# Input projection of a hybrid decoder layer in seven block products for pairs of column tiles, with attention in groups of two query blocks

## The chip, the core and the metric

The kernel runs on one core of a Trainium2 chip. The core's engines each follow their own queue and meet through semaphores: PE (TensorE) multiplies, DVE (VectorE), ACT (ScalarE) and POOL (GpSimd) work elementwise, SP issues DMA transfers. The metric is the device time of one execution in microseconds, the median of the runs.

## The reference, cut to what matters

One layer for 1024 prompt tokens and 32 sample tokens (8 sequences of 4), all in float32. `w_in` has 9472 columns, 74 tiles of 128.

```python
u = rmsnorm(x, norm_pre)
proj = jnp.einsum('bld,de->ble', u, w_in)
aq, af, ai, aog, az, bq, bk, bv, bz, ga, gb = jnp.split(proj, offs, axis=-1)
# branch A: gated linear recurrence, 8 heads of 128 channels
oa, s_new = hgrn2_branch(aq, af, ai, aog, s_hgrn, lb, hgrn_norm)
a = jnp.einsum('ble,ed->bld', oa * silu(az), w_pa)
# branch B: attention over a window of 128, 16 heads, 2 key heads, a sink per head
b = jnp.einsum('ble,ed->bld', swa(bq, bk, bv) * silu(bz), w_pb)
m = sigmoid(ga) * a + sigmoid(gb) * b
x = x + rmsnorm(jnp.einsum('bld,de->ble', m, w_o), norm_post)
x = x + (p @ w_ple) * sigmoid(x @ w_ple_gate)
```

The recurrent states, and the last 128 keys and values, are outputs too.

## The kernel before

Activations lie transposed, channels on partitions: a projection's tile of 128 output columns is a product over eight channel tiles (k). For float32 accuracy each operand is split exactly into a rounded part and a rest (`wh`, `wl`, `uH`, `uL`, type fp32r), and three products are added for each k: wh x uH, wh x uL, wl x uH. `gemm` (line 245 issues all its products) does this for three chunks of 352 tokens, 24 products into one of three PSUM banks each, so 72 a tile; the sample's 32 tokens are the end of the third chunk. The first head's first two tiles run in chunks of 256, 256, 256 and 288 while the tokens still arrive. `weights` loads a tile of 1024 x 128, rounds it on ACT (L216) and subtracts on DVE (L217).

PE's order is written out by hand. Dependent work stands in generators in two queues; `gemm` calls `tick` after each quantum of products (8; 4 in attention), and `tick` lets the first generator of each queue go on to its next `yield`, which says how many quanta it waits. The other engines' orders come from the framework's planner, which starts what is ready and prefers what was written earlier; at run time each engine keeps that order.

The stages: the norm and the turning of the input (`x_rest`, `turn`); for each of eight heads five tiles (f, q, i, og, z) with the head's chain beside them (`hgrn_proj`, `hgrn_chain`, and `turn_v` for the values): pairs of tokens in blocks of 4, 16 and then halves of 32, 64, 128 (L573 to L636), states (L674, L691), outputs (L703, L705), squares (L707), scaled outputs (L717, L718), their transposes (L732). The chain's PSUM is two double banks (`double`) and one single bank (`single`); the values of the sample are spread over sequences by POOL (L686). Then keys and values, with `turn_kv` beside the values' projection; eight gates of branch A in turn with its output projection (`gate_a`, `ep_pa`); for each of eight tiles (two heads each) bq and bz with `attention` beside them; the sample's attention; eight gates of branch B; its projection and the merge; the output projection, post norm, residual and the layer input.

`attention` takes a tile in two halves of four query blocks: logits of two blocks (L884, L888) with the reduction that adds the bias (L893), softmax of four blocks (L904, L909), transposes of the probabilities into two banks `pt` (L929, copies L933 and L935), values into a bank `po` (L956), gating (L962). Its steps wait `A_WAIT` quanta.

Of the kernel before, what the change touches and what calls it, by code (L numbers as in the profile page):

```python
# [11 lines left out]
F32 = mybir.dt.float32  # L12
# [15 lines left out]
A_QUANTUM = 4  # L28
A_WAIT = (5, 4, 4, 5, 5, 4, 3, 3, 3, 3)
# [10 lines left out]
# column offsets of the parts of the input projection  # L40
# [3 lines left out]
# layout of the constant tile (columns)  # L44
# [6 lines left out]
C_SM = 344  # L51
# [10 lines left out]
def _constants():  # L62
    """Tables that depend on shapes alone: identity, masks, one-hot rows of the distance buckets."""
# [3 lines left out]
    # the ten (source, target) pairs of a block of four: columns t=1..3 with s=t, t=2,3 with s=t-1, t=3 with s=1,  # L67
    # and t=0..3 with s=0; then the same of four blocks of four in one of sixteen, and of two halves of 32
# [13 lines left out]
    c[:32, C_VM:C_VM + 8] = tok[:, None] // 4 == np.arange(8)[None, :]  # L82
    b = _buckets()
# [8 lines left out]
    # one-hot rows of the buckets along the reversed distance axis, and a row for what is masked  # L92
# [4 lines left out]
    # the same for the four sample positions: row (t, bucket), column key  # L97
# [14 lines left out]
def tile_decoder_step(ctx: ExitStack, tc: tile.TileContext, x_prompt, x_sample, state_hgrn, cache_k, cache_v,  # L112
# [13 lines left out]
    wp = ctx.enter_context(tc.tile_pool(name="wp", bufs=2))  # L126
    ep = ctx.enter_context(tc.tile_pool(name="ep", bufs=2))
    dp = ctx.enter_context(tc.tile_pool(name="dp", bufs=1, space=DRAM))
    psg = ctx.enter_context(tc.tile_pool(name="psg", bufs=3, space=PSUM))

# [1 line left out]
    oa_d = [dp.tile([P, NTOK], F32, name=f"oa_d{h}") for h in range(NH)]  # L132
    ma_d = [dp.tile([P, NTOK], F32, name=f"ma_d{h}") for h in range(KT)]
# [4 lines left out]
    cst = cp.tile([P, C_W], F32, name="cst")  # L138
# [7 lines left out]
    def rsqrt_steps(dst_i, src, scale, tag, pool_):  # L146
        """dst_i (an int32 tile, read as float32) = (src * scale + EPS) ** -0.5, an instruction a step"""
# [23 lines left out]
    # ---- the order of work on the tensor engine: projections in quanta of a few products, with the steps of  # L171
    # ---- dependent work (generators in queues) between them; a step yields how many quanta to wait, or a condition
# [30 lines left out]
    wn = [0]  # L203

    def weights(srcs, kt=KT, split=True):
        i = wn[0]
        wn[0] += 1
        raw = wp.tile([P, NTOK], F32, name=f"raw{i}", tag="raw")
        raw3 = raw[:, :kt * P].rearrange("p (k m) -> p k m", k=kt)
        for dst, src in srcs:  # L210
            DM.dma_start(dst(raw3), src)
        wh = wp.tile([P, KT, P], F32R, name=f"wh{i}", tag="wh")
        wl = wp.tile([P, KT, P], F32R, name=f"wl{i}", tag="wl")
        if not split:
            return wh, wl, raw3
        S.copy(wh[:, :kt, :], raw3)  # L216
        V.tensor_tensor(wl[:, :kt, :], raw3, wh[:, :kt, :], op=ALU.subtract)  # L217
        return wh, wl

    def w_cols(src, col, kt=KT, split=True):  # L220
        return weights([(lambda r: r, src[:, col:col + P].rearrange("(k p) m -> p k m", p=P))], kt, split)

    def w_strips(src, base, c):
        out = []
        for j in range(2):
            col = base + (c + 8 * j) * 64
            out.append((lambda r, j=j: r[:, :, 64 * j:64 * j + 64], src[:, col:col + 64].rearrange("(k p) m -> p k m", p=P)))
        return weights(out)

    def w_rows(i):  # L230
        return weights([(lambda r, j=j: r[64 * j:64 * j + 64],
                         w_pb[0, 512 * j:512 * j + 512, i * P:(i + 1) * P].rearrange("(k p) m -> p k m", p=64)) for j in range(2)])

    gn = [0]

    def gemm(w, xh, xl, epilogue, kt=KT, chunks=CHUNKS, quantum=8):
        wh, wl = w
        n = 0
        for lo, hi in chunks:
            gn[0] += 1  # L240
            ps = psg.tile([P, 512], F32, name=f"g{gn[0]}", tag="g")[:, :hi - lo]
            sl = slice(lo, hi)
            for k in range(kt):
                for m, (a, b) in enumerate(((wh, xh), (wh, xl), (wl, xh))):
                    T.matmul(ps, a[:, k, :], b(k)[:, sl], start=k == 0 and m == 0, stop=k == kt - 1 and m == 2)  # L245
                    n += 1
                    if n % quantum == 0 and not (k == kt - 1 and m == 2):
                        tick()
            epilogue(lo, sl, ps)
            tick()  # L250
# [4 lines left out]
    # =====================================================================================  # L255
    # input norm, transposed: u^T in two exact float32r parts
    # =====================================================================================
    ap_, ap_es = opened("ap")
    uHt = ap_.tile([P, KT, NTOK], F32R, name="uH", tag="AH")
    uLt = ap_.tile([P, KT, NTOK], F32R, name="uL", tag="AL")  # L260
    uH, uL = rows(uHt), rows(uLt)

    st, st_es = opened("st")
    sps, sps_es = opened("stps", bufs=5, space=PSUM)
    done = set()
    rawt = ep.tile([P, NTOK], F32, name="rawt", tag="ep")
    raws = [rawt[:24, i * P:(i + 1) * P] for i in range(2)]
    rs_i = st.tile([P, 9], I32, name="rs_i", bufs=1)
    tabs = st.tile([P, 2], F32, name="tabs", bufs=1)
    xts = []  # L270

    def load_x(i):
        r = P if i < 8 else 32
        xt = st.tile([P, D], F32, name=f"xt{i}", tag="xt", bufs=7)
        DM.dma_start(xt[:r], x_prompt[0, i * P:(i + 1) * P, :] if i < 8 else x_sample.rearrange("b t d -> (b t) d"))
        xts.append((xt, r))

    # the start's order is by hand on the other engines too
    first = ExitStack()
    first.enter_context(tc.manual_schedule(engines={mybir.EngineType.Activation, mybir.EngineType.DVE, mybir.EngineType.Pool}))  # L280
    one = rawt[:, 768:896]
# [10 lines left out]
    first_w = [w_cols(w_in[0], O_AF, split=False)]  # L292
    load_x(2)
    first_w.append(w_cols(w_in[0], O_AQ, split=False))
    for i in range(3, 9):
        load_x(i)
    DM.dma_start(cst[:, P:], cst_d[:, P:])
    DM.dma_start(sink, attn_sink.broadcast_to([P, 16]))

    def split_w(i):  # L300
        wh, wl, raw3 = first_w[i]
        S.copy(wh, raw3)
        for hf in range(2):
            k = slice(4 * hf, 4 * hf + 4)
            G.tensor_tensor(wl[:, k], raw3[:, k], wh[:, k], op=ALU.subtract)

    def squares(i):
        xt, r = xts[i]
        sq = st.tile([P, D], BF16, name=f"sq{i}", tag="sq")
        S.activation(sq[:r], xt[:r], AF.Square, accum_out=ssq[:r, i:i + 1])  # L310

    def chain(i, n):
        return rsqrt_steps(rs_i[:, i:i + n], ssq[:, i:i + n], 1.0 / D, f"u{i}", st)
# [15 lines left out]
    def turn(p, q, beside=()):  # L329
        """two of the eight channel tiles of a pair of token tiles, times the norm's weight"""  # L330
# [6 lines left out]
        dst = slice(256 * p, 256 * p + 256)  # L337
        gs = [g_pre[:, 2 * q + k:2 * q + k + 1] for k in range(2)]
        for k in range(2):
            S.activation(uHt[:, 2 * q + k, dst], pt[:, k, :], AF.Copy, scale=gs[k])  # L340
# [968 lines left out]
```

## Time and profile before

| | |
|---|---|
| median of 3 runs | 1566.18 us (1565.2 to 1570.24) |
| span of the profiled execution | 1565.5 us |
| one head (from 165.5 to 239.8 us) | 74.3 us |
| one tile of attention (from 861.0 to 897.3 us) | 36.3 us |
| gates and projection of branch A (651.3 to 848.0) | 196.7 us |

A group's line names the source line, engine, operation, output and inputs, shapes and count; behind the bar stand busy time and the mean duration of one in ns, then idle time ahead of them and who ended it. Matmuls overlap in PE, so the distance from start to start says what one costs, and its duration does not. A timeline's line begins with start and duration in us. A window's line gives the stretch, each engine's busy time with its instructions, PE's granted clock, the DMA engines' share and GB/s. A line of waits gives total us, times and the longest.

### The profile page before, as it was taken

How to read it: one execution, taken by the hardware profiler on the slowest of the kernel's cores; microseconds unless marked ns; L12 is line 12 of the kernel's file. 1: busy time of each engine (PE TensorE's matmuls, PEld its weight loads, DVE VectorE, ACT ScalarE, POOL GpSimd, SP SyncE). 2: the span in 40 equal slices, each digit the busy share in tenths (PEclk: the TensorE clock that was granted, in tenths of full speed). 3: DMA queues.
4: the chain of work that ended last, by engine and by line, in shares of the span. 5: the costliest groups of instructions: out<-in, count | busy, mean ns of one | idle time of the engine just before them, and what ended most of it. 6: DMA issues, size and time to landing. Idle time of an engine off the chain costs nothing.

```text
span 1565.5 us, 28202 instructions
## 1 busy us (share of the span) xinstructions
PE 1542.4 (99%) x11799; PEld 1477.2 (94%) x11799; DVE 765.1 (49%) x1875; ACT 520.5 (33%) x1257; POOL 133.6 (9%) x98
## 2 busy tenths in 40 slices
PE   8999999999999999999999999999999999998998
PEld 8999999999999999999999888888999999997998
DVE  7746464646455564421213666666524344227532
ACT  6342323332323323511113444444324112323422
POOL 2211010202020202200000000000000000004100
PEclk9999999999999999999999999999999999998999
DMA  6121212121212121522222111111222454203321
GB/s 201 55 70 42 79 33 84 42 70 42 83 31 82 30 82 31 177 76 69 76 62 75 35 39 39 46 35 37 68 76 76 138 134 127 67 13 117 94 82 56
DMA packets 181578, 112.24 MB, mean 72 GB/s; under 512 B 40003, under 2 KB 174076, under 8 KB 181436
## 3 DMA queue, kind: packets, MB, share of 16 engines
q1 hardware_dynamic: 180636, 110.21, 24.3%
q8 instruction: 92, 1.51, 0.4%
q14 instruction: 34, 0.28, 0.1%
q0 software_dynamic: 672, 0.18, 0.1%
q10 hardware_dynamic: 144, 0.07, 0.0%
HBM read 88.22 MB, written 23.22 MB: 71 GB/s over the span
## 4 chain that ended last, share of the span: by engine, by line
PE 87%; DVE 5%; DMA 3%; issue 2%; ACT 1%; SPq 0%; DVEq 0%; ACTq 0%
PE g L245 72%; DMA mar<-ma_d 3%; PE po L956 2%; PE pt L929 2%; PE lp L884 1%; DVE wl L217 1%; PE d L463 1%; PE d L703 1%; PE d L674 1%; PE lp L888 1%; PE d L705 1%; DVE mL L1112 1%; PE d L573 1%; PE b L636 1%; DVE gbr L1110 0%
## 5 line engine op out<-in xcount | busy, mean ns | idle before, releaser
L245 PE MATMUL g<-uH,wh 128*128 128x352 f32 (+2 forms) x1792 | 583.6, 326 | 0.0
L245 PE MATMUL g<-uL,wh 128*128 128x352 f32 (+2 forms) x1792 | 580.4, 324 | 0.0
L245 PE MATMUL g<-uH,wl 128*128 128x352 f32 (+2 forms) x1792 | 579.6, 323 | 0.0
L245 PEld LDWEIGHTS g<-uL,wh 128*128 128x128 f32 x1792 | 337.9, 189 | 8.8 <-issue 5.2
L245 PEld LDWEIGHTS g<-uH,wh 128*128 128x128 f32 x1792 | 337.4, 188 | 9.3 <-issue 7.2
L245 PEld LDWEIGHTS g<-uH,wl 128*128 128x128 f32 x1792 | 337.5, 188 | 6.2 <-issue 3.4
L217 DVE TENSOR_TENSOR wl<-raw,wh 128x1024 fp32r<-128x1024 f32 (+1 forms) x112 | 135.3, 1208 | 228.2 <-ACT wh L216 228.1
L216 ACT CAST wh<-raw 128x1024 fp32r<-128x1024 f32 (+1 forms) x112 | 112.2, 1002 | 289.8 <-PE g L245 279.2
L1211 POOL TENSOR_TENSOR yT<-yT,acc 128x1056 f32<-128x1056 f32 x4 | 12.9, 3246 | 766.3 <-ACT acc L1207 766.3
L904 ACT ACTIVATE lg<-lg,mx 128x256 f32<-128x256 f32 (+1 forms) x128 | 61.6, 483 | 26.7 <-DVE mx L898 26.6
L893 DVE CUSTOM_DVE_ANT_0 lg<-lp,hank,sink 128x256 f32<-128x256 f32 (+1 forms) x128 | 52.4, 464 | 24.2 <-PE lp L888 23.9
L245 PE MATMUL g<-x1L,wh 128*128 128x352 f32 (+3 forms) x192 | 62.7, 327 | 0.6 <-DVE x1L L1225 0.6
L245 PE MATMUL g<-x1H,wh 128*128 128x352 f32 (+3 forms) x192 | 63.0, 328 | 0.0
L245 PE MATMUL g<-x1H,wl 128*128 128x352 f32 (+3 forms) x192 | 62.9, 327 | 0.0
L245 PE MATMUL g<-obH,wl 128*128 128x352 f32 x192 | 62.5, 326 | 0.0
L245 PE MATMUL g<-oH,wl 128*128 128x352 f32 x192 | 62.4, 325 | 0.0
L245 PE MATMUL g<-mH,wl 128*128 128x352 f32 x192 | 62.4, 325 | 0.0
L245 PE MATMUL g<-obH,wh 128*128 128x352 f32 x192 | 62.2, 324 | 0.0
L245 PE MATMUL g<-oH,wh 128*128 128x352 f32 x192 | 62.1, 324 | 0.0
L245 PE MATMUL g<-mH,wh 128*128 128x352 f32 x192 | 62.1, 323 | 0.0
L245 PE MATMUL g<-oL,wh 128*128 128x352 f32 x192 | 62.0, 323 | 0.0
L245 PE MATMUL g<-obL,wh 128*128 128x352 f32 x192 | 62.0, 323 | 0.0
(319 smaller groups left out, 2317.3 us busy)
## 6 DMA issues: line engine op xcount, KB each, us to landing
raw<-in_w_in_dram SPq DMA_DIRECT2D x58, 512.0 KB
raw<-in_w_in_dram SPq DMA_DIRECT2D x32, 256.0 KB
oa_d<-G SPq DMA_DIRECT2D x8, 528.0 KB
oar<-oa_d SPq DMA_DIRECT2D x8, 528.0 KB
ma_d<-sga SPq DMA_DIRECT2D x8, 528.0 KB
gb_d<-sgb SPq DMA_DIRECT2D x8, 528.0 KB
gbr<-gb_d SPq DMA_DIRECT2D x8, 528.0 KB
mar<-ma_d SPq DMA_DIRECT2D x8, 528.0 KB
```

The costliest lines, as they stand in the source:

```text
L216: S.copy(wh[:, :kt, :], raw3)
L217: V.tensor_tensor(wl[:, :kt, :], raw3, wh[:, :kt, :], op=ALU.subtract)
L245: T.matmul(ps, a[:, k, :], b(k)[:, sl], start=k == 0 and m == 0, stop=k == kt - 1 and m == 2)
L463: T.transpose(b[:, i * P:(i + 1) * P], src[:, i * P:(i + 1) * P], ident)
L573: T.matmul(bA[32 * a:32 * a + 32, P * c:P * c + 80], K[:, s0:s0 + 32], QP[:, s0 // 4:s0 // 4 + 8, :].rearrange("p b j -> p (b j)"), start= ...
L636: T.matmul(bD[:64, 64 * c:64 * c + 64], K[:, c * P:c * P + 64], QE[:, c * P + 64:c * P + 128], start=True, stop=True, tile_position=(0, 0))
L674: T.matmul(b[:, c * P:(c + 1) * P], kn[:, c, :], vn[:, c, :], start=True, stop=True)
L703: T.matmul(o, att[:, c, :], vn[:, c, :], start=True, stop=c == 0)
L893: V.tensor_tensor_reduce(lg[:, j, i, lo:], bs[j][:, os], hank[:, j, ::-1][:, lo:], 1.0, sink[:, c + 8 * j:c + 8 * j + 1], ALU.add, ALU.max ...
L904: S.activation(lg[:, j, i, lo:], lg[:, j, i, lo:], AF.Exp, bias=mx[:, 1, 4 * j + i:4 * j + i + 1], accum_out=mx[:, 3, 4 * j + i:4 * j + i ...
L929: T.transpose(b[:, 256 * j + P * w:256 * j + P * w + P], lgs[hf][:, j, q - 4 * hf, half:half + P], ident)
L956: T.matmul(po[r, col:col + len(qs) * P], vN[:, kb, r], pT[:, j, :len(qs) * P], start=first, stop=last, skip_group_check=True, tile_positio ...
```

## The change

Two column tiles of the projection become a pair. With the channels cut into two halves and the 1024 tokens into two halves of 512, a pair is a 2 x 2 block product, and on three of the four channel tiles of each half (`M` = 3) it is formed with seven block products of sums and differences; the fourth tile of each half (`R` = 2 in all) is multiplied plainly. Each block product still has the three part products, at 512 columns. The input's sums are made once (`difference`: T1 to T4 beside the four blocks), the weights' sums for each pair (`prep`, three products ahead, `AHEAD`). Partial results are copied out of PSUM and added by DVE (`kept`, `out`). The sample's tokens are multiplied by the raw weights in float32, on four column groups (`sample_products`, `sample_outputs`). The first head's f and q stay plain in chunks of 256.

The pairs: f and q, i and og, z and the gate of branch A for a head (so that gate moves into the heads, through DRAM); keys and values; bq and bz for each tile; two gates of branch B. Memory is shared by tags: the chain's buffers serve attention too. The chain's `single` is now half of one of the two double banks, the values turn in three pieces (`turned`), the sample's states are made in two halves. Attention works in four groups of two blocks, with one bank `pt` and one `po`; its outputs go to DRAM. Branch A's projection moves behind the last gates of branch B, over operands (`parts`) that take the memory of the input's variants.

```diff
-A_QUANTUM = 4
-A_WAIT = (5, 4, 4, 5, 5, 4, 3, 3, 3, 3)
+M = 3
+R = 8 - 2 * M
+HT = 512
+QUANTUM = 6
+A_QUANTUM = 3
+A_WAIT = (3, 3, 2, 1, 2)
+AHEAD = 3
...
+    def split(W, key, x, eng, shape, tag, bufs):
+        h = wp.tile(shape, F32R, name=tname("wh"), tag=tag + "h", bufs=bufs)
+        l = wp.tile(shape, F32R, name=tname("wl"), tag=tag + "l", bufs=bufs)
+        S.copy(h, x)
+        eng.tensor_tensor(l, x, h, op=ALU.subtract)
+        W.v[key] = (h, l)
+
+    def prep(W):
...
+        split(W, "P1", a11, G, shape, "w", 4)
+        yield
+        s1 = sums(a21, a22, ALU.add)
+        split(W, "P5", s1, V, shape, "w", 4)
+        yield
+        s2 = sums(s1, a11, ALU.subtract)
+        split(W, "P6", s2, V, shape, "w", 4)
+        yield
+        split(W, "P2", a12, G, shape, "w", 4)
+        if R:
...
+            for i in range(2):
+                S.copy(h[:, i], W.raw[i][:, M:4])
+                V.tensor_tensor(l[:, i], W.raw[i][:, M:4], h[:, i], op=ALU.subtract)
+            W.v["R"] = (h, l)
+        yield
+        s3 = sums(a11, a21, ALU.subtract)
+        split(W, "P7", s3, V, shape, "w", 4)
+        yield
+        G.tensor_tensor(s2, a12, s2, op=ALU.subtract)
+        split(W, "P3", s2, V, shape, "w", 4)
+        yield
+        split(W, "P4", a22, G, shape, "w", 4)
+        yield
...
+    def sample_products(raws, xs):
+        gs = psg.tile([P, 512], F32, name=tname("gs"), tag="gs", bufs=1)
+        for k in range(KT):
+            r = slice(32 * (k % 4), 32 * (k % 4) + 32)
+            T.matmul(gs[r, :2 * P], xs[:, k, :], raws[k // 4][:, k % 4].rearrange("p j m -> p (j m)"), start=k < 4, stop=k >= 4,
+                     tile_position=(0, 32 * (k % 4)))
+        part = gt.tile([P, 2 * P], F32, name=tname("part"), tag="part", bufs=1)
+        S.copy(part, gs[:, :2 * P])
+        return gs, part
...
+        ta, tc_, tb = banks
+        a = bank(ta)
+        product(a, "P1", "B11", True)
+        gs, part = sample_products(W.raw, X.s)
+        c1 = kept("c1", a)
+        c = bank(tc_)
+        product(c, "P5", "T1", True)
+        p5 = kept("p5", c)
+        product(a, "P6", "T2", False)
+        sample_outputs(gs, part, eps)
+        u2 = kept("u2", a)
+        b = bank(tb)
+        product(b, "P2", "B21", True)
+        plain(b, 0, 0, False)
+        out(0, 0, b, c1)
+        product(a, "P7", "T3", False)
+        if R:
+            b = bank(tb)
+            plain(b, 1, 1, True)
+            V.tensor_tensor(p5, b, p5, op=ALU.add)
+        out(1, 1, a, p5)
+        product(c, "P3", "B22", False)
+        plain(c, 0, 1, False)
+        out(0, 1, c, u2)
+        product(a, "P4", "T4", False)
+        plain(a, 1, 0, False)
+        eps[1](0, slice(0, HT), a)
+        banks[:] = [tb, tc_, ta]
+        tick()
...
+    def difference(x, dst, a, b, i, eng):
+
+        (ah, al), (bh, bl), (dh, dl) = ((x.v[n][0][:, i], x.v[n][1][:, i]) for n in (a, b, dst))
+        t, t2 = ctile(), ctile()
+        V.tensor_tensor(t, ah.bitcast(F32), bh.bitcast(F32), op=ALU.subtract)
+        G.tensor_tensor(t2, al.bitcast(F32), bl.bitcast(F32), op=ALU.subtract)
+        V.tensor_tensor(t, t, t2, op=ALU.add)
+        S.copy(dh, t)
+        eng.tensor_tensor(dl, t, dh, op=ALU.subtract)
...
+    def single():
+        return double()[:, :512]
...
+        logits(0)
+        yield A_WAIT[0]
+        logits(1)
+        yield A_WAIT[1]
+        for g in range(4):
+            p0 = turn(g, 0)
+            yield 1
+            p1 = turn(g, 1)
+            yield A_WAIT[2]
+            po = values(g, p0, p1)
+            while g < 2 and ("bz", c) not in done:
+                yield 1
+            gated(g, po)
+            if g < 2:
+                yield A_WAIT[3]
+                logits(g + 2)
+            yield A_WAIT[4]
...
+        pair_gemm(b_pairs[c], u, (ep_bq, ep_bz), quantum=A_QUANTUM)
...
+    oar = load_staged(oa_d, "oar")
+    gate_b(3)
...
+    oH, oL = parts(oar, "o", ap_, ("AH", "AL"))
+    obr = load_staged(ob_d, "obr")
+    obH, obL = parts(obr, "ob", obs, ("OH", "OL"))
```

780 lines of the change are left out of this document (461 added, 319 removed).

## The prediction

> **What bounds the kernel now.** I read the engines' shares first, then the chain that ended last, then what PE waited for.
>
> ```profile
> PE 1542.4 (99%) x11799; PEld 1477.2 (94%) x11799; DVE 765.1 (49%) x1875; ACT 520.5 (33%) x1257; POOL 133.6 (9%) x98
> PE 87%; DVE 5%; DMA 3%; issue 2%; ACT 1%; SPq 0%; DVEq 0%; ACTq 0%
> PE xtp L1218 <- DVE yT L1220: 5.1, 3, 2.4
> PE d L631 <- DVE attD L648: 5.0, 8, 0.6
> ```
>
> PE is busy almost throughout, it is 87% of the chain, and the two longest sums of its waits are 5 us each. So the kernel is the length of PE's queue, which is written out by hand: a step that finds its input late holds everything behind it. What a product costs is read where products follow one another:
>
> ```profile
> L245 PE MATMUL g<-uH,wh 128*128 128x352 f32 x1728 | 564.6, 327 | 0.0
> 183.10 25.64 PE g L245 x160
> ...
> 1544.94 0.33 PE L245 MATMUL g<-x1H,wh 128*128 128x352 f32 x1
> ...
> 1546.73 0.33 PE L245 MATMUL g<-x1H,wl 128*128 128x352 f32 x1
> 1546.89 0.40 PE L245 MATMUL g<-x1H,wh 128*128 128x512 f32 x1
> ...
> 1550.40 0.39 PE L245 MATMUL g<-x1H,wh 128*128 128x512 f32 x1
> ```
>
> The mean of 327 ns is latency; 160 products in the chain took 25.64 us, 0.160 us each. At the end of the kernel eleven steps of 352 columns take 1.79 us (0.163 each) and fifteen of 512 take 3.51 us (0.234): a ratio of 1.438, as the columns have (1.455). In the projection I take 512 columns at 0.231 us, between 0.230 (the rows' ratio) and 0.233 (the columns').
>
> **PE's own work.** A pair of tiles costs 144 x 0.16025 = 23.08 us before. After, seven products of three channel tiles in three part products are 63 and the plain fourth tile adds 4 x 6 = 24: 87 x 0.231 = 20.10 us. That is 2.98 us less. But the 32 sample tokens, which rode in the 352s, become plain float32 work: eight products on four column groups with 256 columns moving, and two more to add the partial sums. The nearest rows are the state products of the sample, eight on four column groups with 128 columns:
>
> ```profile
> 162.97 1.95 PE L674 MATMUL d<-vn,kn 128*128 128x128 f32 x16
> 164.85 0.64 PE L691 MATMUL b<-S,QE 128*32 128x128 f32 x16
> 165.42 0.43 PE L245 MATMUL g<-uH,wh 128*128 128x352 f32 x1
> 165.69 0.32 PE L245 MATMUL g<-uL,wh 128*128 128x352 f32 x1
> ```
>
> L691 holds PE 0.57 us, so twice its columns 1.14. The two sums are four records, each at most the 1.88/16 = 0.12 us of L674: 0.25 to 0.5, I take 0.4. The way back into the projection costs 0.11 us (0.27 to the second product, not 0.16), twice: 0.2. So 1.75 us, and a pair gains 1.23 us; over 36 pairs **-44 us**. The first pair (head 0) stays plain; its 48 products of 288 columns lose 32 columns each (48 x 32 x 0.455 ns = 0.7 us) and it gets the sample: **+1**. The chains break in more often: attention 16 times a tile, not 10, HGRN about 3 times more a head; at 0.15 us (0.11 to 0.2) 72 breaks are **+11**. The gate of branch A only moves into the heads. PE's work falls by **32 us**; with the bounds, by 20 to 40.
>
> **Single waits that come in.** The input's four difference variants (three tiles each) are made behind the last prompt tokens. One is: DVE subtracts 512 columns while POOL subtracts the low parts, DVE adds, ACT rounds, DVE (POOL for the first variant) subtracts.
>
> ```profile
> 228.58 0.68 DVE L642 TENSOR_TENSOR QE<-QE,Tb 128x512 f32<-128x512 f32 x1
> 164.39 0.93 POOL L529 TENSOR_TENSOR G<-G,sz 128x352 f32<-128x352 f32 x1 [10.60 <-issue]
> L216 ACT CAST wh<-raw 128x1024 fp32r<-128x1024 f32 (+1 forms) x112 | 112.2, 1002 | 289.8 <-PE g L245 279.2 <-issue 9.5 <-ACT x1H L1223 0.7
> L217 DVE TENSOR_TENSOR wl<-raw,wh 128x1024 fp32r<-128x1024 f32 (+1 forms) x112 | 135.3, 1208 | 228.2 <-ACT wh L216 228.1
> ```
>
> POOL 512 x 0.93/352 = 1.35, DVE 0.68, ACT half of 1.0, DVE 0.68: 3.2 us. Each takes two of three temporary tiles, so they come one behind the other: variants ready 9.7, 19.4, 29 and 38.7 us after the tokens. PE needs them after 10.4 (two last chunks, the sample, one product), then 12.5, and, thus delayed, 25.4 and 36: waits of 0, 6.9, 3.6 and 2.7, **+13** (5 to 25).
>
> Keys and values are now one pair, and what prepares the distance table, covered by the values' projection before, comes after it: one load and a rounding, **+3** (0 to 6). Branch A's projection comes after the last gate; its split operands take the memory of the input variants and of the gate's temporaries. So the last gate's epilogue and store, then one tile's rounding, then eight subtractions at 1.2 us, lie ahead of 24 products that need 3.9 us. Before, `gate_a(0)` lay over that. A store that the chain shows:
>
> ```profile
> 1225.61 5.42 DMA gb_d<-sgb
> ```
>
> That one moves 528 KB; the last one now is a half, so 2.7 us. 1 + 2.7 + 1.0 + 9.7 - 3.4 = **+11** (6 to 16). Sum of this part **+27**.
>
> **Waits that recur.** Before, a finished bank was needed again two banks later (7.7 us). In the new pair, bank b is wanted again nine products (2.1 us) after the addition that frees it is issued, and bank a 15 products (3.5 us) after two additions. So the answers of DVE must be quick, and it is busier. By stage:
>
> ```profile
> core 0: us, PE busy (x) PEld busy (x) DVE busy (x) ACT busy (x) POOL busy (x), PEclk, DMA share, GB/s
> 165.50:239.80 74.30, 73.67 (x700) 70.98 (x700) 40.69 (x95) 22.90 (x60) 11.44 (x7) 1.00 0.20 59
> 861.00:897.30 36.30, 36.30 (x247) 32.31 (x247) 23.96 (x82) 16.51 (x51) 0.00 (x0) 1.00 0.16 37
> ```
>
> The first row is one head, the second one tile of attention. A pair adds four additions of 512 columns out of PSUM, and smaller weight splits:
>
> ```profile
> 874.31 0.69 DVE L962 SCALAR_TENSOR_TENSOR o<-po,zt 128x512 f32<-128x512 f32 x1 [0.60 <-PE po L956]
> 203.38 1.23 DVE L217 TENSOR_TENSOR wl<-raw,wh 128x1024 fp32r<-128x1024 f32 x1 [3.56 <-ACT wh L216]
> ...
> 215.34 0.29 DVE L591 COPY_PREDICATED attS<-cst,d 32x8 f32<-32x8 int32 x1
> ```
>
> 4 x 0.69 = 2.8, and about 3.1 for four splits of 384 and two of 256 where two of 1024 took 2.4: +3.5 us of DVE a pair. From 203.38 to 215.6 DVE works without a gap: a new answer that falls there waits. POOL gets three splits and four sums of 384 columns a pair, 1.0 us each, 7 us where attention had none. What POOL does to DVE:
>
> ```profile
> 221.50 6.60 POOL L686 TENSOR_TENSOR vS<-vh,cst 32x1024 fp32r<-32x1024 f32 x3 [10.20 <-ACT vh L682]
> 223.97 2.38 DVE L642 TENSOR_TENSOR QE<-QE,Tb 128x512 f32<-128x512 f32 x1
> 180.58 1.85 POOL L529 TENSOR_TENSOR G<-G,sz 128x352 f32<-128x352 f32 x1 [8.95 <-DVE sz L528]
> ```
>
> The same DVE operation takes 2.38 us, not 0.68, while POOL works, and POOL's 1.85, not 0.93, beside DVE. At 0.7 us of delay for each of seven POOL operations, DVE loses about 5 us a pair (0 to 7). [...]
>
> A head: 74.3 + 11.5 (the gate) = 85.8 us before; 3 x 21.85 + 17.0 = 82.6 of PE after. Its waits, with quanta of 1.39 us: the sample's turn wants one of two double banks while the second is held for the halves and the first for masks (2.3); the outputs' transposes come 6.2 us behind the outputs, where squares, roots and scaling need
>
> ```profile
> 172.89 0.28 ACT L707 ACTIVATE junk<-d 128x128 f32<-128x128 f32 x1 [2.88 <-PE d L705]
> 182.06 0.34 ACT L718 ACTIVATE on<-b,ri 32x128 f32<-32x128 f32 x1
> ```
>
> 9.5 (3.0); the second half of the sample's values on POOL (3.3 us for two quanta, 0.5 to 1); the halves and additions on a busier DVE (1.5). That is 7.5; since one wait covers the next I take 6 (1 to 14): 8 heads, **+48**.
>
> A tile of attention: PE 36.3 - 23.1 + 22.8 = 36.0. DVE 24 + 3.5 + 1.7 (four groups of small softmax steps, not two), 29, with POOL's delays 34: almost the period. Its waits: the first turn of a tile follows its logits by 4.6 us, where the softmax of two blocks takes:
>
> ```profile
> L904 ACT ACTIVATE lg<-lg,mx 128x256 f32<-128x256 f32 (+1 forms) x128 | 61.6, 483 | 26.7 <-DVE mx L898 26.6
> L893 DVE CUSTOM_DVE_ANT_0 lg<-lp,hank,sink 128x256 f32<-128x256 f32 (+1 forms) x128 | 52.4, 464 | 24.2 <-PE lp L888 23.9
> L909 DVE TENSOR_SCALAR lg<-lg,mx 128x256 f32<-128x256 f32 (+1 forms) x128 | 34.0, 340 | 0.2
> L935 DVE COPY pT<-pt 128x512 f32<-128x512 f32 (+1 forms) x32 | 19.3, 618 | 10.8 <-PE pt L929 10.7
> ```
>
> Four of each of the first three, with small steps some 6 us, so 1.2 to 4 late; the two turns of a group share one bank with three products (0.7 us) between them and a copy of 0.62 us and its signals on DVE (0.2 to 1.2, four times); the second logits 1.4 us behind the first, whose reductions take 1.9 (0.4 to 1.5). That is 2.4 to 10.3 us; by the DVE row, which leaves it 2 us of spare, I take 8 (2 to 16): 8 tiles, **+64**.
>
> **Sum.** -32 + 27 + 48 + 64 = +107 on the span of 1565.5: 1672.5; the median of the runs lies 0.7 above the span, so **1673 us**.
>
> **Rivals.** *The answers come in time:* DVE has 49% over the span and much that it does in bursts has no due time; if each answer comes within the nine products, only short waits of 0 to 1 us a head or tile stay, and the single waits come at their lower ends (11): -32 + 11 + 0 to 16 = 1545 to 1561, **faster**. Against it stand the 12 us without a gap and one bank for both turns. *DVE or POOL becomes the bound:* with 14 us a head and 16 a tile, -32 + 38 + 112 + 128 = 1812; from about 1760 on. It decides where DVE's 34 us in attention pass PE's 36. [...] *The gain and the waits cancel:* 2 us a head and 2 a tile give 1565.5 - 32 + 11 + 32 = 1576 and, a little less, no change.
>
> **How the numbers follow.** Waits of 3 to 12 us a head or tile, 1571 to 1760 with 1673 the likeliest: 0.72. Faster by more than 0.3% (about what a measurement of this kernel can tell from no change): 0.14. Within 0.3%, 1561.5 to 1571: 0.04. DVE or POOL as the bound, above 1760: 0.10. So faster 0.14, same 0.04, slower 0.82. The range of 1555 to 1760 leaves out some 0.09 below and 0.10 above.
>
> **What would show it.** Right: products of 512 columns 0.231 us apart; some 1.75 us of sample work a pair; PE waiting for DVE and ACT at the turns, the outputs' transposes and the sums, PE's share well under 99%; POOL's operations beside stretched ones of DVE; a gap near 11 us ahead of branch A's projection. Wrong: a head near 83 us and a tile near 36 (waits hidden), 512 columns far from 0.231, or a sample under 1 us.

## The result, and the profile after

| | before | after |
|---|---|---|
| median | 1565.69 us | 1730.45 us (1726.87 to 1731.77) |
| span of the profiled execution | 1565.5 us | 1724.6 us |
| mean granted PE clock | 0.994 | 0.952 |

The changed kernel takes 1.1045 times the time of before (95% interval 1.1024 to 1.1065): slower, as forecast, inside the range of 1555 to 1760 and 57 us above the 1673 that was named. The page of the changed kernel, its shares, the granted clock in 40 slices and the chain:

```profile
PE 1553.3 (90%) x10551; PEld 1282.1 (74%) x10551; DVE 996.6 (58%) x2266; ACT 658.9 (38%) x1649; POOL 422.9 (25%) x390
...
PEclk9879998999999999999999999999989999999999
...
PE 67%; DVE 20%; issue 5%; ACT 5%; POOL 2%; DMA 1%; DVEq 0%; SPq 0%; ACTq 0%; POOLq 0%
```

PE has 1248 instructions fewer and is still busy 11 us longer. Its share fell from 99 to 90%, and DVE holds 20% of the chain where it held 5. What PE waited for, in the view of waits:

```profile
PE d L692 <- DVE attS L846: 41.3, 7, 5.9
PE d L987 <- ACT on L980: 34.5, 8, 4.3
PE d L692 <- DVE attD L845: 22.4, 1, 22.4
PE d L953 <- POOL vS L950: 11.2, 8, 1.4
PE pt L1141 <- DVE pTs L1145: 10.7, 27, 0.9
PE pt L1141 <- DVE lg L1131: 9.7, 8, 1.4
PE g L1369 <- ACT oH L1379: 6.9, 1, 6.9
```

Seven rows, 137 us. The lines of the new code: L692 is the turning of values (`turned`), which needs a double bank that the masked pairs (L842 to L846) still hold; L987 the transposes of a head's outputs; L953 products of the sample's values; L1141 attention's `turn`; L1369 the products of the last stages, here the first of branch A's projection. The first four rows belong to the heads, and there the time went. One product of the chain occurs once a head for the prompt and the sample (one row of each kernel, for heads 1 to 7: count, shortest, median and longest in ns, start of the first and the last):

```profile
L575 PE MATMUL d<-QP,K x14: 232/232/233, 135.5 to 581.3; 128*32 128x80 f32 x14
```

```profile
L830 PE MATMUL d<-QP,K x14: 232/233/233, 193.9 to 780.7; 128*32 128x80 f32 x14
```

With these marks the spans split in three. A gate of branch A moved into each head (72 products, 11.5 us), and the projection moved to the end; the gates are taken out of the difference.

| stretch | before | after | difference without the moved gates | forecast |
|---|---|---|---|---|
| start to head 1 | 135.5 | 193.9 | +47 | +17 |
| head 1 to head 7, six heads | 445.8 | 586.8 | +72 | +17 |
| head 7 to the end | 984.2 | 943.9 | +40 | +73 |

The forecast's column is its own terms laid on the same marks: 2.8 us a head (82.6 + 6 - 85.8), 13 for the input's variants and 1 for the first pair in the first row, and the rest of the +107 in the last. So the sum on the span was 52 us short, with two rows too low (30 and 55) and one too high (33). What a head and a tile look like inside, from the view of windows (a head, a tile, then a stretch behind one wait and the start of branch A's projection):

```profile
194.00:292.00 98.00, 86.37 (x651) 67.17 (x649) 59.06 (x120) 36.35 (x96) 33.57 (x32) 0.93 0.19 56
895.00:934.00 39.00, 36.15 (x218) 25.47 (x217) 28.43 (x94) 20.54 (x65) 7.06 (x7) 1.00 0.20 48
255.00:258.00 3.00, 0.00 (x0) 0.00 (x0) 1.19 (x5) 2.04 (x9) 0.00 (x0) 0.98 0.01 3
258.00:261.00 3.00, 2.81 (x11) 2.32 (x12) 0.73 (x1) 0.32 (x2) 0.00 (x0) 0.50 0.00 0
261.00:264.00 3.00, 3.00 (x20) 1.08 (x19) 1.15 (x3) 1.08 (x3) 0.00 (x0) 0.50 0.02 5
1276.00:1283.00 7.00, 0.15 (x1) 0.00 (x0) 1.65 (x2) 2.67 (x4) 0.00 (x0) 0.67 0.79 229
1283.00:1294.00 11.00, 10.27 (x27) 7.26 (x28) 10.92 (x10) 11.00 (x13) 0.00 (x0) 0.50 0.97 349
```

A head leaves PE about 11.6 us idle and has a clock of 0.93; a tile leaves it 2.9 us idle at full clock. The fourth row (258 us) and the last show what the prediction had no term for: behind a stand of 4.3 or 7 us PE ran at half its clock (0.50). In the timeline of the same stretch, beside the same work one pair later:

```profile
258.19 1.97 PE L987 MATMUL d<-cst,on 128*128 128x128 f32 x8 [4.33 <-ACT on L980]
...
261.91 1.94 PE L348 MATMUL gs<-raw,xs 128*32 128x256 f32 x16
...
284.64 1.07 PE L348 MATMUL gs<-raw,xs 128*32 128x256 f32 x16
```

The sample's products take 1.94 us at half clock (0.50 from 261 to 264 us) and 1.07 at full (1.00 from 280 to 290 us).

The first head stands longest, in another place than forecast. Its PE waits 22.45 us for masked pairs, which DVE has queued behind the input's differences (9.5 us of it, by DVE's timeline) and behind weights and the chain's own steps (PE's timeline, then three rows of DVE's; L473 is the last step of a difference):

```profile
104.61 0.37 PE L692 MATMUL d<-cst,ts 128*32 128x128 f32 x1 [22.45 <-DVE attD L845]
```

```profile
80.30 0.68 DVE L473 TENSOR_TENSOR LT<-ct,HT 128x512 fp32r<-128x512 f32 x1
...
95.02 1.48 DVE L473 TENSOR_TENSOR LT<-ct,HT 128x512 fp32r<-128x512 f32 x1
...
104.02 0.44 DVE L845 COPY_PREDICATED attD<-cst,d 128x64 f32<-128x64 int32 x1
```

### The profile page after: what moved, and what is told of

The parts are those of the page before. It is cut to its first block, busy times and chain, and to the rows that moved or that the text cites. A ratio compares the mean times of both kernels' runs of the same rounds, so it can differ in the third digit from the quotient of the medians.

```text
span 1724.6 us, 27936 instructions
## 1 busy us (share of the span) xinstructions
PE 1553.3 (90%) x10551; PEld 1282.1 (74%) x10551; DVE 996.6 (58%) x2266; ACT 658.9 (38%) x1649; POOL 422.9 (25%) x390
## 4 chain that ended last, share of the span: by engine, by line
PE 67%; DVE 20%; issue 5%; ACT 5%; POOL 2%; DMA 1%; DVEq 0%; SPq 0%; ACTq 0%; POOLq 0%
PE g L366 30%; PE g L1369 22%; DVE lg L1118 2%; PE gs L348 2%; DVE QE L852 1%; PE po L1156 1%; POOL vS L950 1%; DVE ct L399 1%; ACT on L980 1%; DVE wl L266 1%; PE pt L1141 1%; PE d L987 1%; DVE lg L1131 1%; ACT lg L1126 1%; PE d L967 1%
## 5 line engine op out<-in xcount | busy, mean ns | idle before, releaser
L366 PE MATMUL g<-HT,wh 128*128 128x512 f32 x432 | 186.2, 431 | 1.9 <-ACT wh L265 1.9
L366 PE MATMUL g<-HT,wl 128*128 128x512 f32 x432 | 173.1, 401 | 4.9 <-DVE wl L266 4.9
L266 POOL TENSOR_TENSOR wl<-raw,wh 128x384 fp32r<-128x384 f32 x108 | 115.8, 1075 | 239.6 <-ACT wh L265 120.6
L366 PE MATMUL g<-LT,wh 128*128 128x512 f32 x432 | 173.2, 401 | 0.0
L265 ACT CAST wh<-ws 128x384 fp32r<-128x384 f32 x144 | 73.6, 512 | 217.7 <-PE g L366 211.7
L366 PE MATMUL g<-HB,wh 128*128 128x512 f32 x324 | 141.7, 437 | 0.0
L366 PE MATMUL g<-HB,wl 128*128 128x512 f32 x324 | 129.6, 400 | 0.0
L366 PE MATMUL g<-LB,wh 128*128 128x512 f32 x324 | 129.2, 399 | 0.0
L366 PE MATMUL g<-HR,wrh 128*128 128x512 f32 x288 | 123.4, 428 | 0.0
L366 PE MATMUL g<-HR,wrl 128*128 128x512 f32 x288 | 116.6, 405 | 0.0
L366 PE MATMUL g<-LR,wrh 128*128 128x512 f32 x288 | 116.1, 403 | 0.0
L366 PEld LDWEIGHTS g<-HT,wh 128*128 128x128 f32 x432 | 84.8, 196 | 38.6 <-issue 13.9
L265 ACT CAST wh<-raw 128x384 fp32r<-128x384 f32 x108 | 55.7, 516 | 124.1 <-PE g L366 57.1
L366 PEld LDWEIGHTS g<-HT,wl 128*128 128x128 f32 x432 | 83.7, 194 | 25.0 <-DVE wl L266 6.0
L366 PEld LDWEIGHTS g<-LT,wh 128*128 128x128 f32 x432 | 84.6, 196 | 14.1
L366 PEld LDWEIGHTS g<-HB,wh 128*128 128x128 f32 x324 | 62.6, 193 | 15.3 <-issue 3.4
L366 PEld LDWEIGHTS g<-HB,wl 128*128 128x128 f32 x324 | 62.5, 193 | 14.5
```

The lines of the kernel that those rows point to most:

```text
L265: S.copy(h, x)
L266: eng.tensor_tensor(l, x, h, op=ALU.subtract)
L366: T.matmul(ps, a, b, start=start, stop=stop, skip_group_check=True)
```

## The experiments

The theory after these readings: the kernel is slower because some steps of PE's queue come before their input, three in each head, and each such stand costs the wait and then some 2 us at half clock. The rivals: DVE is so full that a moved step only uncovers the next wait; or PE's own work, with the sample's float32 products, is no less than before.

**One step later, two times, and the stand filled.** e1_turn puts the sample's turn five quanta later, e2_tail the outputs' transposes six. e3_warm leaves every step and puts 16 products of the identity, which nothing reads, into the stand ahead of the transposes.

```diff
e1_turn
-            enqueue(turned(sl, ps, vn, ("v", h)), 2, q=1)
+            enqueue(turned(sl, ps, vn, ("v", h)), 7 if sl.start == NP else 2, q=1)
e2_tail
-        yield 2
+        yield 8
         while ("z", h) not in done:
e3_warm
             yield 1
+        gw = psg.tile([P, 512], F32, name=tname("gs"), tag="gs", bufs=1)
+        for _ in range(16):
+            T.matmul(gw[:, :P], ident, ident, start=True, stop=True)
         b = double()
```

> The changed kernel (1730 us) with one number changed: the turning of the sample's values waits 7 quanta behind its product, not 2, so that PE asks for the double bank after DVE has read the masks' bank. Theory A (the shared bank is the cause, and PE's clock drops behind so long a wait): the 41 us recorded there for heads 1 to 7 go and 2 to 3 us a head of slow clock with them, 45 to 65 us in all, about 1675. Theory B (DVE is late as such, so the next step that needs it waits instead): under 20 us, above 1710, and PE's waits only move to other rows. Theory C (waits alone cost, the clock doesn't matter): 35 to 41 us, about 1690.

> The changed kernel with the transposes of a head's outputs 8 quanta behind the outputs at the least, not 2. Theory A: the 34.5 us that PE waits for ACT there go, and some 3 us a head of half clock behind it: 45 to 60 us, about 1675. Theory B (the work is only put off and meets the next head's steps): under 20 us. Theory C (waits alone): 30 to 35 us, about 1697.

> The changed kernel with 16 products of the identity (3.9 us of PE, read by nobody) ahead of the transposes of a head's outputs, in the time in which PE waits 4.3 us for ACT. If the clock falls because PE stands still, PE keeps its full clock and the work behind runs faster: 3 us a head, 15 to 26 us in all, about 1708, though PE does more. If the slow work behind the wait has another cause, no change: 1728 to 1735.

Measured: e1_turn 1697.04 us (1.0831 of before, 1.0814 to 1.0848), e2_tail 1684.13 (1.0747, 1.0731 to 1.0763), e3_warm 1713.24 (1.0930, 1.0911 to 1.0949): 33, 46 and 17 us less than the changed kernel. The largest wait of e1_turn, then the new one of e2_tail:

```profile
PE g L366 <- DVE ct L399: 38.0, 8, 16.8
```

```profile
PE g L366 <- ACT c L392: 10.1, 8, 1.3
```

In e1_turn the 64 us of L692 are gone, and 38 of them are back at L366: the bank that an addition frees (`out`, L399) is wanted before it is free, the wait that the prediction named for bank b and gave a part of 1.5 us a head. One stand of 16.8 us among them is the first head's: there the 22.4 us mostly changed their place, and head 1 starts at 193.7 us where it was 193.9. The time is nearest to the third theory's 1690, but not for its reason, since part of the waits came back. In e2_tail 34.5 us of waits went, 10.1 came, and the time fell by 46: more than the difference of the waits. e3_warm says why. The stretch of the timeline that follows the same stand as above:

```profile
257.48 1.09 PE L990 MATMUL d<-cst,on 128*128 128x128 f32 x8 [0.74 <-ACT on L980]
...
259.56 1.07 PE L348 MATMUL gs<-raw,xs 128*32 128x256 f32 x16
260.56 0.50 PE L366 MATMUL g<-HT,wh 128*128 128x512 f32 x1
```

Nothing arrives sooner there, but PE does 128 products more and the kernel is 17 us faster. From the transposes to the end of the sample's products PE takes 3.08 us (257.48 to 260.56) where it took 5.59 (258.19 to 263.78 in the changed kernel): 2.5 us a head, 20 for eight heads. So the lower clock is a cost of its own, 2 to 2.5 us for each of these stands of 4.3 us (17 and 20 us over eight heads).

**All steps of the heads at once.** e4_heads has e1 and e2, the second half of the sample's values two quanta later, and the first head's chain 12 quanta later.

```diff
-            yield 2
+            yield 2 + 2 * g
             b = single()
...
-        enqueue(hgrn_chain(h, F4, QP, K, vn, Gt), 2)
+        enqueue(hgrn_chain(h, F4, QP, K, vn, Gt), 2 if h else 14)
```

> The two later steps together, the second half of the sample's values four quanta behind the first, not two, and the first head's chain 14 quanta behind its projection, not 2, so that the input's differences come ahead of it on DVE. Theory A: the gains add, 90 to 120 us for the two, about 10 for the values, 15 to 25 for the first head: 1580 to 1615. Theory B (DVE's work takes its time wherever the steps stand): above 1660.

Measured 1635.33 us (1.0436, 1.0421 to 1.0452), 95 less than the changed kernel and between its two cases. The marks of the heads, and the largest wait that is left:

```profile
L830 PE MATMUL d<-QP,K x14: 232/233/233, 189.0 to 697.6; 128*32 128x80 f32 x14
```

```profile
PE g L366 <- DVE ct L399: 30.4, 7, 11.0
```

A head takes (697.6 - 189.0) / 6 = 84.8 us where it took 97.8. The first head's later chain won little: head 1 starts at 189.0, where e2_tail alone has 188.7. One window of 40 us tells why, for the changed kernel, e4_heads and e8_plain (below, which makes no differences):

```profile
65.00:105.00 40.00, 11.89 (x99) 8.55 (x100) 39.99 (x52) 9.85 (x21) 23.45 (x16) 0.65 0.09 27
65.00:105.00 40.00, 20.70 (x58) 14.33 (x59) 38.62 (x48) 9.73 (x21) 23.93 (x16) 0.63 0.09 26
65.00:105.00 40.00, 38.42 (x302) 29.03 (x303) 10.41 (x20) 8.37 (x15) 1.29 (x1) 0.93 0.18 53
```

DVE (the third busy time) works 39.99 and 38.62 of the 40 us, and 10.41 without the differences. So in the heads the theory holds, and in the first head the first rival: there a moved step uncovers the next wait.

The next four each change one thing of e4_heads. e5_gs gives the plain product of (1,1) the sample's bank; e6_pool lets DVE make what POOL made of the weights; e7_attn gives attention's second logits and second turn a quantum more; e8_plain multiplies all four blocks of a pair plainly, with everything computed and nothing summed.

```diff
e5_gs
-            b = bank(tb)
+            b = psg.tile([P, 512], F32, name=tname("gs"), tag="gs", bufs=1)
             plain(b, 1, 1, True)
e6_pool
-        split(W, "P1", a11, G, shape, "w", 4)
+        split(W, "P1", a11, V, shape, "w", 4)
...
-            G.tensor_tensor(s, a, b, op=op)
+            V.tensor_tensor(s, a, b, op=op)
e7_attn
-A_WAIT = (3, 3, 2, 1, 2)
+A_WAIT = (3, 4, 2, 1, 1)
...
-            yield 1
+            yield 2
             p1 = turn(g, 1)
e8_plain
+        for t in range(2):
+            for j in range(2):
+                a = bank(banks[0])
...
+                    for m, (p, q) in enumerate(((wh, xh), (wh, xl), (wl, xh))):
+                        mm(a, p, q, k == 0 and m == 0, k == KT - 1 and m == 2)
```

> Against e4_heads (1635): the plain product of (1,1) goes into the sample's bank in place of the bank that (0,0) has just left. Theory (PE is held by the addition that frees that bank, 30 us in 7 waits, with the clock behind them): the waits of L366 on DVE's L399 go, 1595 to 1608. Rival (the addition itself is late because DVE has too much work in the heads): the same waits come back at P7 or P4, which need a bank too, and the time stays within 1625 to 1640.

> Against e4_heads (1635): the weights' sums and subtractions that POOL made (seven operations a pair) are made by DVE. Theory A (POOL's work slows DVE's beside it, some 2.4 us a pair in the heads): DVE's own operations get shorter, the heads' DVE time grows by less than the 5 us a pair of added work, 1625 to 1640. Theory B (DVE's load is what is late, and POOL took load from it at little cost): added waits of PE in every head and tile, 1655 to 1690.

> Against e4_heads (1635): attention's second logits and its second turn of each group get one quantum more, and the end of the group one less. Theory (the waits of L1141 on the copy L1145, 11 us, and on the softmax, 10 us, are steps written too early): these waits go, 1618 to 1626. Rival (attention waits because DVE has 28 of 39 us to do in each tile): the waits move to another step, 1630 to 1640.

> Against e4_heads (1635): the pairs stay, with 512 columns, float32 sample products and the changed order of heads and attention, but each of the four blocks is multiplied plainly: 96 products in place of 87 a pair and no sums or differences of weights, inputs or results. If PE's own work sets the time, 36 pairs x 9 products x 0.227 us = 74 us come in and the waits on sums (about 30 us, and those of the first head, 20 us) go: 1650 to 1690. If the sums' load on DVE, ACT and POOL is what holds the kernel up, the waits that go outweigh the nine products: below 1620.

| | median, us | to before | against e4_heads |
|---|---|---|---|
| e5_gs | 1605.98 | 1.0244 (1.0227 to 1.0261) | -29 |
| e6_pool | 1604.85 | 1.0242 (1.0227 to 1.0258) | -30 |
| e7_attn | 1626.68 | 1.0377 (1.0361 to 1.0392) | -9 |
| e8_plain | 1655.07 | 1.0560 (1.0544 to 1.0577) | +20 |

e5_gs came as its theory said: the wait on the addition fell from 30.4 to 3.8 us, and only some 4 us of it came back (at L859). e7_attn, just above its theory's 1626, lowered attention's waits at L1141 from 20.6 to 4.3 us, and 12.6 us stood up at the next step, the values:

```profile
PE po L1156 <- ACT pTs L1145: 12.6, 14, 1.4
```

e8_plain came out within the range that PE's work gave: nine products more a pair are 74 us, and 54 came back in waits and slow work that went. Its marks of the heads, and two of its waits:

```profile
L786 PE MATMUL d<-QP,K x14: 232/233/233, 163.2 to 694.0; 128*32 128x80 f32 x14
```

```profile
PE g L1322 <- ACT wh L1300: 16.7, 1, 16.7
PE g L1322 <- DVE wl L1301: 6.7, 1, 6.7
```

Up to head 1 it is 26 us sooner than e4_heads (163.2 against 189.0), since the differences are gone; a head takes 88.5 us where it took 84.8. The two waits lie ahead of branch A's projection: 23.4 us, where e4_heads has 8.8 (6.9 and 1.9). So some 15 of the 20 us are a longer stand there, whose cause is open, and not products: with the waits of e4_heads the seven products are worth some 5 us of their 74, an estimate.

e6_pool was expected by neither theory: 30 us less, though DVE has 252 operations more. The groups of DVE's view by lines, e4_heads first, then e6_pool:

```profile
L266 DVE TENSOR_TENSOR wl<-ws,wh 128x384 fp32r<-128x384 f32 x144 | 100.5, 699 | 60.9 <-ACT wh L265 59.8
L1118 DVE CUSTOM_DVE_ANT_0 lg<-lp,hank,sink 128x256 f32<-128x256 f32 x112 | 48.9, 480 | 22.6 <-PE lp L1114 22.6
```

```profile
L266 DVE TENSOR_TENSOR wl<-ws,wh 128x384 fp32r<-128x384 f32 x144 | 91.1, 633 | 42.6 <-ACT wh L265 39.1 <-PE pt L1141 2.7
L1118 DVE CUSTOM_DVE_ANT_0 lg<-lp,hank,sink 128x256 f32<-128x256 f32 x112 | 48.4, 481 | 17.0 <-PE lp L1114 16.9
```

The subtraction that reads two operands from SBUF got shorter (699 to 633 ns), the reduction whose operand lies in PSUM did not (480 and 481). The busy times on the page of e6_pool, and what is left of the wait that held 30.4 us in e4_heads:

```profile
PE 1520.8 (95%) x10551; PEld 1261.1 (79%) x10551; DVE 1033.3 (64%) x2518; ACT 652.9 (41%) x1649; POOL 169.3 (11%) x138
```

```profile
PE g L366 <- DVE ct L399: 6.2, 6, 1.2
```

DVE's busy time is 50 us more than in e4_heads (983.3). The durations of its operations, which overlap a little, add up to 73 us more (1094 and 1167), and the 252 operations taken from POOL last 147 of them: so beside POOL's 258 us of work (427.3 less 169.3) DVE's own operations had lasted some 74 us longer. With them shorter the addition can come sooner: 24 us of its wait are gone, and 8 stand up at the rounding of weights (L265). An operation with one small SBUF operand got shorter too (L1120, 298 to 165 ns); what sets which operations POOL's work lengthens no run shows.

**Together, and two things more.** e9_all has e5, e6 and e7 on e4. e10_diff and e11_warm each add one edit to it: the low half of an input difference lies in its result's place and not in a second temporary tile; and 24 products that nothing reads stand ahead of branch A's projection.

```diff
e10_diff
-        t, t2 = ctile(), ctile()
+        t = ctile()
...
-        G.tensor_tensor(t2, al.bitcast(F32), bl.bitcast(F32), op=ALU.subtract)
-        V.tensor_tensor(t, t, t2, op=ALU.add)
+        G.tensor_tensor(dl, al.bitcast(F32), bl.bitcast(F32), op=ALU.subtract)
+        V.tensor_tensor(t, t, dl.bitcast(F32), op=ALU.add)
e11_warm
     gate_b(3)
+    gw = psg.tile([P, 512], F32, name=tname("gs"), tag="gs", bufs=1)
+    for _ in range(24):
+        T.matmul(gw[:, :P], ident, ident, start=True, stop=True)
```

> The edits of e5_gs, e6_pool and e7_attn together, on e4_heads (1635). e5_gs gave -29 and e6_pool -30, and in both the waits on the addition L399 went, so the two may be one gain: then 1588 to 1598. If POOL's work also cost elsewhere (first head, other operations of DVE), both add up: 1565 to 1578.

> Against e9_all: the low half of an input difference lies in the place of its result and not in a second temporary tile, so three differences are in flight and not one and a half. Theory (the differences of the first head follow one another because of the temporaries, with ACT's rounding between them): PE's waits from 65 to 91 us shrink, 8 to 20 us less than e9_all. Rival (DVE's load in the first head sets it): within 4 us of e9_all.

> Against e9_all: 24 products that nothing reads are put on PE where it stands before branch A's projection (about 7 us idle, then about 10 us at a lower clock). Clock theory: the projection then starts at full clock, 2 to 6 us less than e9_all although nothing arrives sooner. Rival (the projection's first products wait for their operands anyway): within 1.5 us of e9_all, or later by what the 24 products run past the wait.

Measured: e9_all 1585.25 us (1.0112, 1.0093 to 1.0131), between its two cases: the gains of e5, e6 and e7 alone add to 68, together they are 50, so some 18 us were the same wait. Its heads, by the marks and by one window of 81 us:

```profile
L830 PE MATMUL d<-QP,K x14: 232/232/233, 180.5 to 664.0; 128*32 128x80 f32 x14
```

```profile
275.00:356.00 81.00, 81.00 (x660) 64.19 (x659) 60.58 (x141) 35.20 (x97) 13.30 (x10) 1.00 0.22 67
```

A head now is 80.6 us of PE without a gap at full clock, DVE 60.6 of them busy. With the moved gate it took 85.8 before: the new head gains 5.2 us once nothing stands. Against e8_plain's 88.5, of which 1.6 are a wait, it is 6.3 us less; 27 products, nine in each of three pairs, are 6.1.

e10_diff took 1591.80 us (1.0156, 1.0139 to 1.0174), 7 more than e9_all, and e11_warm 1585.08 (1.0127, 1.0109 to 1.0145), the same. Both theories fell, and of the rivals only that of e11_warm held. With three differences in flight POOL's subtractions lie beside an almost unbroken row of DVE's, which is busy 23.84 of the 25 us from 65 us on (POOL's timeline, then PE's, of e10_diff):

```profile
70.29 12.37 POOL L470 TENSOR_TENSOR LT<-LB,LT 128x512 fp32r<-128x512 f32 x3 [4.88 <-DVE LT L473]
```

```profile
86.68 0.79 PE L366 MATMUL g<-HT,wh 128*128 128x512 f32 x1 [19.91 <-ACT wh L265]
```

Three of them take 12.37 us, where one takes 1.65 in e9_all. The first alone, in the chain that ended last:

```profile
70.29 9.48 POOL LT L470
```

The additions, the weights of the next pair and PE stand behind it: the engine whose operation gets longer here is POOL. In e9_all, where DVE is as busy (23.84 of the same 25 us), it is DVE: beside a subtraction of 1.65 us on POOL, its own of 384 columns takes 1.61 us, where it takes 0.54 without. What decides between the two is open. In e11_warm the clock held through the stand (1.00 from 1135 to 1140 us and 0.81 in the next 5, where e9_all has 0.87 and 0.50), but the projection's first products are paced by the rounding of their operands, one tile of ACT and DVE after another, and its clock falls there (the timeline, then one window):

```profile
1133.96 5.52 PE L1323 MATMUL gs<-cst 128*128 128x128 f32 x48
1141.27 0.43 PE L1372 MATMUL g<-oH,wh 128*128 128x352 f32 x1 [1.79 <-ACT oH L1382]
```

```profile
1145.00:1150.00 5.00, 5.00 (x13) 3.50 (x14) 5.00 (x5) 5.00 (x7) 0.00 (x0) 0.50 0.96 323
```

A warm clock was worth something where the work behind a stand was ready, as in e3_warm (17 us), and nothing where it was not (1585.08 us here, 1585.25 in e9_all).

**The last try.** e12_best adds three edits to e9_all: differences wholly on DVE, low halves in place; attention's quanta of two products; branch B's operands rounded behind the second tile of branch A's projection.

```diff
-A_QUANTUM = 3
-A_WAIT = (3, 4, 2, 1, 1)
+A_QUANTUM = 2
+A_WAIT = (4, 5, 4, 1, 1)
...
-        G.tensor_tensor(t2, al.bitcast(F32), bl.bitcast(F32), op=ALU.subtract)
+        V.tensor_tensor(dl, al.bitcast(F32), bl.bitcast(F32), op=ALU.subtract)
...
+        if i == 1:
+            obr = load_staged(ob_d, "obr")
+            obH, obL = parts(obr, "ob", obs, ("OH", "OL"))
```

> Against e9_all (1585): the input differences wholly on DVE with the low half in place of the result, attention's quanta of two products in place of three with one more of them ahead of the values, and branch B's operands rounded behind the second tile of branch A's projection instead of ahead of it. Theory (what is left of the loss lies in three places, each a step that is late, with the clock behind it): the first head gives 6 to 12, attention's waits for the copies 6 to 12, the projection's second gap 3 to 6; 1555 to 1570, level with the kernel before or just under it. Rival (each wait that goes uncovers the next, or DVE in the first head gets later without POOL): 1576 to 1590.

Measured 1590.23 us (1.0155, 1.0142 to 1.0169): the rival, at its upper end. Two rows of its waits, then the start of the projection in PE's timeline, and the same start in e9_all:

```profile
PE g L366 <- ACT wh L265: 18.3, 1, 18.3
...
PE psc L1246 <- DVE sx L1240: 3.9, 1, 3.9
```

```profile
1151.75 0.66 PE L1369 MATMUL g<-oH,wh 128*128 128x352 f32 x1 [5.75 <-ACT oH L1379]
```

```profile
1140.22 0.66 PE L1369 MATMUL g<-oH,wh 128*128 128x352 f32 x1 [6.60 <-ACT oH L1379]
```

The differences are done sooner, but the next pair's weights now stand behind all of them on DVE, and one wait of 18.3 us takes the place of several: by the mark of head 7 (663.2 against 664.0) 0.8 us is won. The projection starts 11.5 us later and the span is only 3.0 longer (1588.4 to 1585.4): what comes from there on is 8.5 us shorter, so the later rounding of branch B's operands seems to have helped. The 11.5 us came in between, where the sample's attention now lies: at 1114 us PE waits 3.9 us for its softmax (the row of L1246), and its granted clock is 0.62 and 0.70 in the two stretches of 10 us from 1110 on, where e9_all has 1.00. That it starts later because attention's finer quanta leave more of the last tile over is argued, not shown. e9_all with the late rounding alone was not tried; by these numbers, an estimate, it would take some 1577. No version here is faster than the kernel before.

## Why the prediction held, and where its sizes were off

- **What bounds the kernel** was right: the length of PE's queue, in which a late step holds everything. Every edit that only moved steps (e1, e2, e4, e7) changed the time, by what PE then waited for and by the slow work behind it.
- **PE's own work, -32 us**, was right in sign and a little small. The forecast had 82.6 us a head and 36.0 a tile; without gaps a head takes 80.6 (e9_all), and a tile of the changed kernel has 36.2 us of PE in a window of 39. The sample's products take 1.07 us where 1.14 were worked out, and 23 steps of 512 columns 5.22 us (1270.55 to 1275.77), 0.227 each and not 0.231. The heads of e8_plain and e9_all show that the nine products saved a pair are real (6.3 us a head for 6.1).
- **The heads, 6 us of waits each**, were mis-sized, by the largest share: 97.8 - 80.6 = 17.2 us. The places were the ones that the prediction listed: the sample's turn behind the masks (forecast 2.3, measured 5.9), the transposes (3.0; 4.3), the sample's values on POOL (0.5 to 1; 1.4). Their sum is 11.6, where the forecast had about 6 for these three: most of that is the sample's turn, 3.6 us too low, and then the transposes, 1.3. They add up, because each stands at its own place in the queue. So two steps failed: "since one wait covers the next I take 6", which took off 1.5 us, and more than that the sizes of the waits themselves. The other 5.6 us have no term: work at half clock behind the two longer stands. PE's busy time agrees, 86.4 us in a head of the changed kernel and 80.6 in e9_all.
- **The additions that free a bank, with the halves 1.5 us a head**, could not show in the changed kernel, where other waits gave DVE time; with those gone they were 38 us (e1_turn) and 30 (e4_heads). This is the one place where a wait had covered the next.
- **The input's variants, +13**, were mis-sized and misplaced. Part of the +47 up to head 1 is one stand of 22.45 us, not of the second pair's products but for the first head's masked pairs, queued behind the differences on DVE. The forecast set the differences' time against the products that read them, and not against the other work that waits for DVE, which is full there (39.99 of 40 us).
- **Attention, 8 us a tile**, was too high: seven tiles run from 890.41 to 1164.79 in the next rows, 39.2 us each where it was 36.3, so 2.9.

```profile
890.41 0.62 PE L1110 MATMUL lp<-KK,stk 128*128 128x128 f32 x4
...
1164.79 0.62 PE L1110 MATMUL lp<-KK,stk 128*128 128x128 f32 x4
```

  DVE has 28.4 of 39 us to do there. The forecast was 29, and 34 with POOL's delays; those 5 us a pair are the term that failed, and with them the argument that DVE has no spare. In e6_pool a tile has 30.2 us of DVE with seven operations more, 28.1 in e4_heads: POOL's delays are 1 to 2 us a tile, an estimate. Attention's reduction, with an operand in PSUM, takes 480 ns with POOL's work (e4_heads) and 481 without (e6_pool).
- **Branch A's projection, +11**: a stand of 6.9 us, then 11 us at half clock for 27 products that take 4.3 at 0.16 us: 13.6 us, near the forecast and inside its 6 to 16. The half clock was no part of it.
- **The rivals.** The answers did not come in time; DVE was not the bound (58% busy), the first head aside. That the waits and the gain cancel is near to what e9_all reaches after seven edits, 20 us above the span of before: by the marks, -31 us over six heads, +34 up to head 1 and +18 behind head 7 (180.5 and 664.0 against 135.5 and 581.3, gates taken out).
- **The range**: its lower bound does not follow from its words. 3 us a head or tile give 1592 with the single waits at their lower ends (1565.5 - 32 + 11 + 48), not 1571. The measured time lies far from that end.

So the 1673 came near to the 1730 by errors of opposite sign, heads and start too low and attention too high, and not because each part was sized well: that the sum came so near is luck.

## What to carry to other kernels

A change that saves products in a queue written by hand is worth its saving only where every step's input has arrived: list each step that follows its input more closely than before, and add the waits up rather than letting one cover the next. Count a stand like the 4.3 us here as the stand plus 2 to 2.5 us of slow work behind it. Look for the stretch in which another engine is full, as DVE is in the first head: moving steps gains little there. Before work goes to POOL, look at what DVE runs beside it: here POOL's help with the weights cost more than it gave (e6_pool, without it, is 30 us faster), while the input's differences moved off POOL (e12_best) gave 0.8 us by the mark of head 7, as the next weights on DVE were then late.

## What the runs showed of the hardware that was not expected

- The granted clock of PE fell to 0.50 behind stands of 4.33 us and of 7 us in the changed kernel, and was 1.00 in its attention from 895 to 1012 us, where the stands are at most 1.4 us; in e11_warm it fell to 0.50 (1145 to 1150 us) behind several short stands, the longest 1.79 us. A stand filled with products that nothing reads kept it up (e3_warm: 1.07 us, not 1.94, for the same 16 products).
- POOL and DVE lengthened each other's operations, both ways: a DVE operation on two SBUF operands (L473 of the changed kernel) took 1.48 us beside POOL and 0.68 without, and POOL's subtraction of 512 columns took 9.48 us in e10_diff beside an almost unbroken row of DVE's, and 1.65 in e9_all, where DVE's operation beside it was the one that lasted longer (1.61 us and 0.54 without).
